# Query and pool-mix products of a decoder trunk as quads of seven block products, interleaved one quad at a time with the attention's units

## The chip, the cores and the metric

The kernel runs on one core of a Trainium2 chip. The metric is the device time of one execution in microseconds (us), the median of several runs. TensorE (PE) multiplies, VectorE (DVE), ScalarE (ACT) and GpSimd (POOL) do elementwise work, SyncE (SP) issues most of the transfers, and 16 DMA engines carry them.

## The reference

One layer with `x` of 2048 tokens by 1024 channels, all in fp32. `c` gives shift, scale and gate through `w_ada`. Then

```
u = x * (1 + scale) + shift
[q | k | v | attn_gate | pool_in | pool_gate | merge_a | merge_p] = u @ W_in
A = SlidingWindowGQA_with_sinks(q, k, v; T5 relative bias) * SiLU(attn_gate)   -> @ W_attn_proj
P = (GroupLinear(MultiScaleCausalPool(pool_in)) * pool_scale) * SiLU(pool_gate) -> @ W_pool_proj
y = (sigmoid(merge_a) * A + sigmoid(merge_p) * P) @ W_out * (1 + gate)
x = LayerNorm(alpha * x + y)
```

The attention has 16 query heads of 64 channels and 2 key heads, with a window of 128 keys that is computed in blocks of 128. The pool averages over the last 2, 4, 8 or 16 tokens, a window for each quarter of the channels.

## The kernel before, in words

**Products.** Every fp32 operand is split into a high part (a copy to fp32r) and a low part (what is left), and a block product is three matmuls for each of four k-tiles: high by high, high by low, low by high (`mm3`, `product`). One block product is thus 12 matmuls of 128x512. A `Quad` is a pair of weight tiles against 1024 tokens. Done plainly it is eight block products; with sums and differences of the blocks (seven products named B11, T1, T2, B21, T3, B22, T4) it is seven. The token side of these seven lies in SBUF as seven sets (`sets`, 2 MB each, high and low). The weight side is a tile `W` of four blocks and a tile `A22`, 1 MB together, which GpSimd turns into sums in place (`sum1` L294, `mid` L298 and L299, `late` L303). ACT and DVE then split them into `w_set` (`pair_split` L325, `half_split` L332, `low` L132), which has four buffers.

**Stages.** The tokens are worked in two halves of 1024, s = 0 and 1. For each half there is a ring (`first_phase` or `second_phase`, run by `ring`) and then an `attention` stage. The ring makes 17 quads two at a time: sixteen gate quads (attn_gate, pool_gate, merge_a, merge_p) and the quad of keys and values. It ends with `first_q`, the plain product of the first query tile. The ring's clock is the tick, one for each block product; `hooks` hang side work on ticks, and a gate's store is put off by two ticks (`defer(2, ...)` in `gate_quad`). At last comes the stage `mix`: attention projection and pool projection of both halves, and the output product with the LayerNorm.

**Attention.** `attention` runs 64 units (head pair by block of 128 queries): scores on PE, bias and maximum on DVE, exponent on ACT, transposes and values on PE. In units 0 to 59 PE also makes half of a plain projection of one 128-channel tile against 512 tokens (`projection`, `parts`): the queries of the next head pair and the pool-mix product. These are plain products, with eight k-tiles and the token sets B11, B21, B22 and, in the set named T2, the raw block B12. The weights of the mix product (`pool_in` folded with the pool's group matrix by `fold_parts`) are kept in DRAM already split (`wmix_d`). Units 60 to 66 open the two quads that the next stage goes on with (`fill_one`). The sums of the pool (`pool_sums`) and the seven block sums of the attention's and the pool's result (`finish`) are made on GpSimd in this stage.

**Side work.** `sums_to` makes the seven sets of the next operand: it loads four blocks into two `spare` rooms, makes four differences on GpSimd, and for each set splits a 128x512 block on ACT (`k_hi`) and DVE (`k_lo`) and stores both (`kept_parts`). `k_hi`, `k_lo`, the gates' `sig` and some others share the five buffers of the tag `c`. In the first ring it does so for the second token half (`u1_d`), in the second ring for `w_out` (`wo_d`), and there `resplit` splits the attention's result of the first half (`ain0_d`). `fill_set` (1 MB a transfer) and `planned` bring sets back. Engines written as `act`, `dve`, `pool`, `sp`, `pe` keep their program order among themselves; `nc.*` calls may be moved by the scheduler.

## Time and profile before

| | us |
|---|---|
| median of 3 runs | 1756.62 (1755.88 to 1757.32) |
| span of the profiled execution, first to last instruction | 1751.3 |
| PE busy | 1697.7 (97%) |
| DVE, ACT, POOL busy | 1205.2, 934.0, 798.3 |
| data moved | 381.31 MB, mean 218 GB/s |

The profiled execution has no other time than its span. The page gives busy time by engine; a view of windows gives the same for a stretch of the span, with the granted clock of TensorE (PEclk, 1.00 is full) and the mean busy share of the 16 DMA engines. Columns of a line that groups instructions: line of the kernel, engine, operation, written and read tiles, shapes, count, busy time, mean of one in ns, and the idle time in front of them with what ended it. Line L56 is that of a helper that keeps the order, so tiles tell the operations apart.

### The profile page before, as it was taken

Reading aid. Unit: us, or ns where it says so; the run is one execution under the profiler, and the core shown is the slowest. Engines: PE = TensorE matmul, PEld = TensorE weight load, DVE = VectorE, ACT = ScalarE, POOL = GpSimd, SP = SyncE. Lnnn points to the kernel's source line nnn. Section 1 sums busy time; section 2 is a strip of 40 time slices with the busy share of each in tenths; the row PEclk is TensorE's granted clock in tenths of the full one; section 3 lists DMA queues with packets and bytes.
Section 4 is the critical chain, followed back from the end, with each engine's and each line's share of the span. In section 5 each row is a group of like instructions: output and inputs, shape, how many; then the busy total and the mean of one; then the engine's idle time right before and its main releaser. Section 6 shows DMA issues by size and latency. Waiting matters only on the chain.

```text
span 1751.3 us, 24998 instructions
## 1 busy us (share of the span) xinstructions
PE 1697.7 (97%) x8248; PEld 1427.4 (82%) x8248; DVE 1205.2 (69%) x2178; ACT 934.0 (53%) x1973; POOL 798.3 (46%) x618
## 2 busy tenths in 40 slices
PE   6899999999999998999999999999999999999996
PEld 5688888878888887888788888888888878887785
DVE  5977665655777777767645357777768696865777
ACT  4644444545777776545444367777745353423452
POOL 2154444441356567434424124555773572463542
PEclk9999999999999999999999999999999999999999
DMA  9384758743354558687777634544698675699432
GB/s 365 117 283 177 276 204 280 257 155 132 114 169 142 178 187 318 237 284 255 276 265 257 234 111 133 180 140 157 232 351 289 185 265 194 216 341 360 157 139 102
DMA packets 185843, 381.31 MB, mean 218 GB/s; under 512 B 18785, under 2 KB 39281, under 8 KB 185713
## 3 DMA queue, kind: packets, MB, share of 16 engines
q1 hardware_dynamic: 179072, 363.92, 59.7%
q0 software_dynamic: 3552, 11.56, 1.7%
q10 hardware_dynamic: 3088, 4.23, 0.8%
q8 instruction: 65, 1.06, 0.2%
q14 instruction: 66, 0.53, 0.1%
HBM read 244.35 MB, written 138.44 MB: 219 GB/s over the span
## 4 chain that ended last, share of the span: by engine, by line
PE 42%; POOL 3%; DVE 2%; DMA 2%; issue 1%; ACT 1%; POOLq 0%; SPq 0%; DVEq 0%; ACTq 0%
PE mm L56 25%; PE lg L56 14%; PE pv L56 2%; PE pt L56 1%; DMA set_T<-ain_T_split 1%; DVE w_set L132 1%; POOL nxt L56 1%; POOL W L298 0%; DVE wide L56 0%; POOL p L56 0%; POOL wide L601 0%; DMA W<-in_wap_dram 0%; POOL rs L56 0%; ACT L L56 0%; POOL a L56 0%
## 5 line engine op out<-in xcount | busy, mean ns | idle before, releaser
L56 PE MATMUL mm<-set_B,w_set 128*128 128x512 f32 x3240 | 799.0, 395 | 12.6 <-ACT u L376 6.3
L56 PEld LDWEIGHTS mm<-set_B,w_set 128*128 128x128 f32 x3240 | 603.2, 189 | 140.7 <-DVE w_set L132 8.8
L56 PE MATMUL lg<-set_T,w_set 128*128 128x512 f32 x2088 | 504.4, 392 | 11.8 <-DVE w_set L132 5.1
L56 PEld LDWEIGHTS lg<-set_T,w_set 128*128 128x128 f32 x2088 | 391.3, 188 | 99.5 <-DVE w_set L132 8.0
L132 DVE TENSOR_TENSOR w_set<-W,w_set 128x1024 fp32r<-128x1024 f32 x162 | 224.0, 1383 | 182.7 <-ACT w_set L325 172.1
L325 ACT CAST w_set<-W 128x1024 fp32r<-128x1024 f32 x162 | 170.6, 1053 | 291.1 <-PE mm L56 221.6
L56 PE MATMUL mm<-set_T,w_set 128*128 128x512 f32 x1080 | 265.6, 394 | 0.0
L56 PEld LDWEIGHTS mm<-set_T,w_set 128*128 128x128 f32 x1080 | 200.7, 188 | 41.1
L294 POOL TENSOR_TENSOR W<-W,A 128x512 f32<-128x512 f32 x56 | 83.8, 1497 | 218.3 <-DMA W<-in_win_dram 59.4
L303 POOL TENSOR_TENSOR W<-W 128x512 f32<-128x512 f32 x56 | 83.5, 1492 | 165.5 <-DVE w_set L132 150.3
L56 DVE TENSOR_TENSOR o<-pv,o 64x128 f32<-64x128 f32 x256 | 72.4, 283 | 88.6 <-ACT o L56 85.5
L56 ACT ACTIVATE L<-L,nm 128x257 f32<-128x257 f32 (+1 forms) x256 | 127.7, 501 | 9.4 <-DVE nm L56 3.9
L298 POOL TENSOR_TENSOR W<-W 128x512 f32<-128x512 f32 x56 | 90.9, 1624 | 78.6 <-DVE w_set L132 68.9
L56 DVE CUSTOM_DVE_ANT_0 L<-lg,bt,nsink 128x256 f32<-128x256 f32 (+1 forms) x256 | 111.6, 473 | 5.0 <-PE lg L56 0.8
L299 POOL TENSOR_TENSOR W<-W 128x512 f32<-128x512 f32 x56 | 88.6, 1582 | 33.6 <-DMA W<-in_win_dram 26.6
L56 POOL TENSOR_TENSOR w_set<-W,w_set 128x1024 fp32r<-128x1024 f32 x14 | 33.7, 2410 | 139.7 <-ACT w_set L56 97.0
L56 POOL TENSOR_TENSOR p<-nxt,pg 128x512 f32<-128x512 f32 x32 | 41.9, 1311 | 107.0 <-DVE sm L56 104.6
L56 ACT COPY o<-pv 64x256 f32<-64x256 f32 x128 | 47.5, 371 | 76.7 <-PE pv L56 76.0
L56 DVE TENSOR_TENSOR ptl<-pt,pth 128x512 fp32r<-128x512 f32 (+1 forms) x128 | 85.8, 670 | 1.9 <-ACT pth L56 1.7
L56 PE MATMUL lg<-kk,qs 128*128 128x256 f32 (+1 forms) x512 | 80.5, 279 | 0.0
L56 ACT ACTIVATE L<-L,sm 128x256 f32<-128x256 f32 (+1 forms) x128 | 64.5, 504 | 30.0 <-DVE sm L56 30.0
L56 DVE TENSOR_TENSOR k_lo<-spare,k_hi 128x512 fp32r<-128x512 f32 x61 | 60.4, 992 | 28.5 <-ACT k_hi L56 13.4
(216 smaller groups left out, 2308.2 us busy)
## 6 DMA issues: line engine op xcount, KB each, us to landing
W<-in_win_dram SPq DMA_DIRECT2D x48, 512.0 KB, 5.2
w_set<-wmix_d SPq DMA_DIRECT2D x32, 512.0 KB, 5.2
W<-in_win_dram SPq DMA_DIRECT2D x34, 256.0 KB, 3.2
A<-in_win_dram SPq DMA_DIRECT2D x34, 256.0 KB, 5.0
ag_d<-sig SPq DMA_DIRECT2D x32, 256.0 KB, 3.9
pg_d<-sig SPq DMA_DIRECT2D x32, 256.0 KB, 3.8
ma_d<-sig SPq DMA_DIRECT2D x32, 256.0 KB, 3.9
mp_d<-sig SPq DMA_DIRECT2D x32, 256.0 KB, 3.8
```

Of the source, the lines that this page charges most:

```text
L56: return lambda *args, **kw: self.tc.keep_in_program_order(op(*args, **kw))
L132: engine.tensor_tensor(dst, src, as32(hi), ALU.subtract)
L294: e.tensor_tensor(self.w[:, 1, :], self.w[:, 2, :], self.a22, ALU.add)
L298: e.tensor_tensor(x[:, 1, :], x[:, 1, :], x[:, 0, :], ALU.subtract)
L299: e.tensor_tensor(x[:, 2, :], x[:, 0, :], x[:, 2, :], ALU.subtract)
L303: e.tensor_tensor(x[:, 3, :], x[:, 3, :], x[:, 1, :], ALU.subtract)
L325: a.copy(by_two(hi), raw)
```

## The change

The plain projections are gone. The query and mix products become quads of seven block products with the sets that the gates use, so that the set T2 stays what it is and B12 is not kept.

- **Ring.** It now makes 10 quads in five groups: eight of attn_gate and pool_gate, the keys and values, and the first query quad. All side work of the rings is placed on these fewer ticks. In the second ring the side work is that of `w_out` as before, the split sums of the attention result of half 0 (`ain0_d`) and the unsplit sums of the pool result (`pin_d[0]`), twelve runs of `sums_to` in all, with eight rooms and starts from tick 3 to 62.
- **Attention.** 13 quads (`fills`: four mix, three query, four merge_a, two merge_p) and the first two products of two more quads are made between the units, in quarters of a block product: 93 products over 67 units, 5 or 6 quarters a unit. The split of each weight block is one 128x512 copy on ACT and one difference on GpSimd, issued three products ahead. Merge gates are stored raw, and their sigmoid is taken when they are read in the last stage. The results of attention and pool are stored raw; their block sums are made later by `sums_to`.
- **After the attention.** The last two merge_p quads (`post`) open a ring of their own, in which the next sets come in (`planned`). T3 and T4 stay in place through the attention.
- **Keys and values.** Only one key head is held at a time; the other lies in DRAM (`k_d`, `v_d`) and is fetched at units 28 to 33.
- **Last stage.** It begins with the two `post` quads of half 1, and eight runs of unsplit `sums_to` for half 1 are spread over its first ticks.
- **Mix weights** are stored unsplit (4 MB in place of 8 MB) by SP in place of GpSimd.

The core of the diff:

```diff
-    def sums_to(ph, store, i, load, work, b12):
-
-        b = []
+    def sums_to(ph, store, i, load, work=None):
+
+        b, split_too = [], store["B11"].shape[0] == 4
...
+        raw = () if not split_too else ((4, "B11", (0, 0)), (5.4, "B21", (1, 0)), (6.1, "B22", (1, 1)))
         for at, name, z in (
-            (4, "B11", (0, 0)), (4.7, "B12", (0, 1)), (5.4, "B21", (1, 0)), (6.1, "B22", (1, 1)),
-            (8.5, "T1", (0, 1)), (10, "T2", (1, 1)), (11.5, "T4", (1, 0)), (13, "T3", (0, 0)),
+            *raw, (8.5, "T1", (0, 1)), (10, "T2", (1, 1)), (11.5, "T4", (1, 0)), (13, "T3", (0, 0)),
         ):
-            if b12 or name != "B12":
+            if split_too:
                 split, keep = kept_parts(ph, store[name][i], lambda z=z: x(*z))
                 todo += [(at, split), (at + 1, keep)]
+            else:
+                todo.append((at + 0.6, lambda name=name, z=z: put(sp, store, name, i, x(*z))))
         return sorted(todo, key=lambda t: t[0])
...
+    def load_raw(store, i):
+
+        def load(x, r):
+            for c in range(2):
+                sp.dma_start(cols(x, c), store[(("B11", "B12"), ("B21", "B22"))[r][c]][i // 2, :, i % 2, :])
+
+        return load
...
+        def block(self, name):
+
+            if name == "T4":
+                return self.a22
+            return self.w[:, {"B11": 0, "T1": 1, "T2": 1, "B21": 3, "T3": 2, "B22": 3}[name], :]
...
-        quads = [kv] if s else []
-        for name, base, kind in (("ag", TAG, "silu"), ("pg", TPG, "scaled"), ("ma", TMA, ""), ("mp", TMP, "")):
+        g = {}
+        for name, base, kind in (("ag", TAG, "silu"), ("pg", TPG, "scaled"), ("ma", TMA, "raw"), ("mp", TMP, "raw")):
             for m in range(0, KT, 2):
-                quads.append(gate_quad(s, name, base, m, kind))
-        last = quads[15:] if s else [kv, quads[15]]
-        return [quads[i : i + 2] for i in range(0, 14, 2)] + [quads[14:15], last], turn
+                g[name, m] = gate_quad(s, name, base, m, "" if (name, m) in (("mp", 4), ("mp", 6)) else kind)
+        def row(name, *ms):
+            return [g[name, m] for m in ms]
+
+        ring_groups = [row("ag", 0, 2), row("ag", 4, 6), row("pg", 0, 2), [kv, q_quad(0)], row("pg", 4, 6)]
+        x = {n: [mk(m) for m in range(0, KT, 2)] for n, mk in (("mix", mix_quad), ("q", q_quad))}
+        ma, mp = row("ma", 0, 2, 4, 6), row("mp", 0, 2)
+        fills = [
+            ("mix", 0, x["mix"][0]), ("ma", 0, ma[0]), ("q", 2, x["q"][1]), ("mix", 2, x["mix"][1]),
+            ("ma", 2, ma[1]), ("q", 4, x["q"][2]), ("mix", 4, x["mix"][2]), ("ma", 4, ma[2]), ("mp", 0, mp[0]),
+            ("q", 6, x["q"][3]), ("mix", 6, x["mix"][3]), ("ma", 6, ma[3]), ("mp", 2, mp[1]),
+        ]
+        return ring_groups, fills, row("mp", 4, 6), turn
...
+        def take_p(m, t, acc):
+            n = pool_free[0] = max(now_n[0], pool_free[0] + 1)
+            x = []
+
+            def first():
+                x.append(ld("pg", gates_d["pg"][s, m, t], 2))
+                x.append(pool_sums(m, t, acc))
+
+            def second():
+                pg, p = x
+                dve.scalar_tensor_tensor(p, p, 1.0 / POOL_W[m // 2], acc, ALU.mult, ALU.subtract)
+                pool.tensor_tensor(p, p, pg, ALU.mult)
+                later(n + 2, lambda: keep_raw(pin_d[s], m, t, p))
+
+            later(n + 1, second)
+            if (m % 2, t) == (0, 1):
+                free_b[0] = n + 1
+            if n == now_n[0]:
+                first()
+            else:
+                later(n, first)
...
+        seq = []
+        for x in range(K):
+            seq += [(x, "T2"), (x, "B21"), (x, "T3"), (x, "B22"), (x + 1, "B11"), (x, "T4"), (x + 1, "T1")]
+        seq += [(K + 1, "B11"), (K + 1, "T1")]
+        splits = {}
+        for i in range(len(seq)):
+            lead = 2 if seq[i] == (K + 1, "B11") else 3
+            splits.setdefault(i - lead, []).append(i)
...
+        def split(i):
+            x, name = seq[i]
+            q = quads[x]
+            if name == "B11" and x > 1:
+                q.sum1(pool)
+            w = ph.split()
+            hi, lo = made[i] = w[:, 0:CH], w[:, CH:]
+            act.copy(hi, q.block(name))
+            low(pool, lo, q.block(name), hi)
+            if name == "T1":
+                q.mid(pool)
+            elif name == "B21":
+                q.late(pool)
+
+        def begun(i):
+            x, name = seq[i]
+            if name == "T1":
+                st[x][1] = bank()
+                if x < K:
+                    later(free_b[0], lambda: seed(x))
+                    if free_b[0] < now_n[0]:
+                        run_coming()
+            if name == "B11":
+                st[x] = [bank(), None, None, None]
+                if x < K:
+                    quads[x + 1].load(ph, False, sp, None)
+            if (x, name) == (K - 1, "B22"):
+                quads[K + 1].load(ph, False, sp, None)
+            for j in splits.get(i, ()):
+                split(j)
+
+        def seed(x):
+            st[x][2] = bank()
+            act.copy(st[x][2], st[x][0])
+
...
+        def filling():
+            for i, (x, name) in enumerate(seq):
+                begun(i)
+                w = made.pop(i)
+                acc = st[x][{"B11": 0, "B21": 0, "T1": 1, "B22": 1}.get(name, 2)]
+                for k in range(4):
+                    product(acc, w, name, name in ("B11", "T1"), k, k + 1)
+                    yield
+                ended(i)
...
-            i = n // 2
-            if i < len(slots):
-                kind, m, st = slots[i]
-                if n % 2 == 0:
-                    accs[kind, m, st], parts[i] = projection(us[st])
-                parts[i](tiles[i // 2][1:], 4 * (n % 2), 4 * (n % 2) + 4)
-            elif n >= 60:
-                fill_one(n)
+            while done < -(-total * (n + 1) // (N + 3)):
+                next(fill)
+                done += 1
...
-        halves_of = [(name, half) for name in set_names[:-1] for half in range(2)]
+        side = []
         for i in range(4):
             ks = (i, 4 + i)
-            todo = sums_to(
+            side.append(sums_to(
                 ph,
                 wo_d,
                 i,
                 lambda x, r, ks=ks: load_wo(x, ks[r]),
                 lambda x, r: dve.tensor_tensor(x, x, cb, ALU.mult),
-                False,
-            )
-            steps(hooks, groups, 5 + 26.5 * i, todo)
-            for n in range(4):
-                if halves_of:
-                    steps(hooks, groups, 19 + 26.5 * i + 2.6 * n, resplit(ph, *halves_of.pop(0)))
-        for half in range(2):
-            hooks.setdefault((-1, 3 + half), []).append(lambda half=half: fill_set("T2", half, u1_d["B12"]))
-        return ring(ph, groups, opened, hooks, [], lambda tick: first_q(ph), True)
+            ))
+        for raw, split in ((ain_d[0], ain0_d), (pin_d[0], pin_d[0])):
+            for i in range(4):
+                side.append(sums_to(ph, split, i, load_raw(raw, i)))
+        ahead, hooks = hooks, {}
+        for start, todo in zip((3, 8, 12, 16, 20, 24, 28, 32, 36, 40, 57, 62), side):
+            for offset, f in todo:
+                at = int(start + offset) - 14
+                if at < 0:
+                    ahead.setdefault((0, at + 14), []).append(f)
+                else:
+                    hooks.setdefault((at // 14, at % 14), []).append(f)
+        later_hooks, hooks = hooks, ahead
+        hooks.setdefault((0, 2), []).append(gate_rows)
+        planned(hooks, ph, u1_d, True)
+        opened = ring(ph, [post], opened, hooks, groups[0], lambda tick: [front(ph, q, tick) for q in groups[0]])
+        hooks = later_hooks
+        planned(hooks, ph, None, False)
+        hooks.setdefault((3, 0), []).append(lambda: ph.turns.clear())
+        turned(hooks, lambda i: turn(ph, i), 4)
+        opened_by = [q for _, _, q in fills[:2]]
+        return ring(ph, groups, opened, hooks, opened_by, lambda tick: [front(ph, opened_by[0], tick)])
...
+        every = [(i, gi) for i, (groups, _) in enumerate(phases) for gi in range(len(groups))]
+        sides = [{} for _ in phases]
+        for n, (raw, i) in enumerate((raw, i) for raw in (ain_d[1], pin_d[1]) for i in range(4)):
+            for offset, f in sums_to(ph, raw, i, load_raw(raw, i)):
+                at = int(2 + 7.5 * n + offset)
+                i, gi = every[at // 14]
+                sides[i].setdefault((gi, at % 14), []).append(f)
...
+    with Pools("g1", spare=4, p=2, c=5) as ph:
+        kq, k, v = rooms_of("second")
+        ph.turns["spare"] = cycle([None, None, *kq, cols2(k, 0), cols2(k, 1)])
+        opened = second_phase(ph, opened, plans[0][2], plans[1])
```

More of the change, by code (lines that the diff above doesn't have):

```diff
@@ L784, in bias_tile, with attention, ld @@
+    def attention(ph, s, fills, post, opened):
+        tp = ph.t
+        run_due(True)
+        quads = [q for _, _, q in fills] + post
+        K = len(fills)
+        def ld(name, src, bufs):
+            x = tp.tile([P, CH], F32, tag=name, bufs=bufs, name=name)
+            sp.dma_start(x, src)
+            return x
         def bias_tile(j):
@@ L922, in attention @@
-        for n in range(N + 5):
+        seed(0)
+        p5 = st[0][3] = tp.tile([P, CH], F32, tag="p5", bufs=2, name="p5")
+        act.copy(p5, st[0][1])
+        for i in range(-3, 0):
+            for j in splits.get(i, ()):
+                split(j)
+        fill = filling()
+        lgs, exps, Ls, pvs, outs, ags = {}, {}, {}, {}, {}, {}
+        total, done = 4 * len(seq), 0
+        for n in range(N + 3):
+            now_n[0] = n
             j, t, b = n // U, n // NB % 2, n % NB
```

517 lines of the change are left out of this document (220 added, 297 removed).

## The prediction

> **What bounds the kernel now.** I read the page first (busy time, costliest groups), then a view of windows by stage, then the chain that ended last, then the transfers.
>
> ```profile
> span 1751.3 us, 24998 instructions
> L56 PE MATMUL mm<-set_B,w_set 128*128 128x512 f32 x3240 | 799.0, 395 | 12.6 <-ACT u L376 6.3
> L56 PE MATMUL lg<-set_T,w_set 128*128 128x512 f32 x2088 | 504.4, 392 | 11.8 <-DVE w_set L132 5.1
> L56 PE MATMUL mm<-set_T,w_set 128*128 128x512 f32 x1080 | 265.6, 394 | 0.0
> ```
>
> The span is 1751.3 us, 5.3 us below the median of the runs (1756.62). I take these 5.3 us as lying around the span and unchanged. The three groups hold 3240 + 2088 + 1080 = 6408 matmuls, 534 block products. Now by stage (columns: length, busy time of PE, PEld, DVE, ACT, POOL, clock, share of the DMA engines, GB/s):
>
> ```profile
> 100.00:413.00 313.00, 310.09 (x1447) 256.99 (x1446) 190.06 (x202) 138.28 (x209) 131.44 (x99) 1.00 0.65 227
> 686.00:700.00 14.00, 7.70 (x29) 6.01 (x28) 6.92 (x11) 5.42 (x9) 10.05 (x10) 0.76 1.00 379
> 700.00:1006.00 306.00, 304.53 (x1346) 251.56 (x1345) 183.39 (x200) 145.52 (x223) 113.68 (x76) 1.00 0.73 258
> 1006.00:1275.00 269.00, 269.00 (x1533) 235.41 (x1532) 193.74 (x605) 199.34 (x587) 137.51 (x107) 1.00 0.50 162
> 1275.00:1325.00 50.00, 49.76 (x233) 41.07 (x232) 30.52 (x47) 21.45 (x38) 29.64 (x25) 1.00 0.91 339
> 1550.00:1600.00 50.00, 50.00 (x222) 41.40 (x221) 26.19 (x25) 12.04 (x15) 23.62 (x18) 1.00 1.04 395
> ```
>
> PE is busy throughout: 310 of 313 us in the first ring, 304.5 of 306 in the second, all of 269 in the second attention. So a block product that goes away is worth its PE time, as long as the others keep up. What matters for them is the last two columns: the second ring already moves 258 GB/s, and the most that 50 us show is 395 GB/s, with the DMA engines busy throughout.
>
> ```profile
> 893.52 2.72 PE lg L56 x12
> 1069.07 2.75 PE mm L56 x12
> 1073.22 2.77 PE mm L56 x12
> ```
>
> From the chain: a block product takes 2.72 us in a ring, 2.75 beside the attention, and a unit of the attention 4.15 us (1073.22 - 1069.07), so 1.40 us of it are the unit's own matmuls.
>
> **What goes: 16 products.** For each token half the queries and mix tiles were 64 plain products (60 in the units, 4 in `first_q`). As eight quads they are 56. Twice 8 products by 2.72 us is **-43.5 us** (518 products, 6216 matmuls). The units' own work stays, and so does the folding.
>
> **The handover after the first attention.**
>
> ```profile
> 686.40 2.91 PE L56 MATMUL lg<-set_T,w_set 128*128 128x512 f32 x12
> 695.61 5.73 PE L56 MATMUL mm<-set_B,w_set 128*128 128x512 f32 x17 [6.30 <-ACT u L376]
> ```
>
> PE idles 6.3 us there, and the next 17 matmuls take 5.73 us instead of 17 x 2.72/12 = 3.85, in the window whose clock is 0.76: 8.2 us in all. T3 and T4 now stay in place, so this wait goes. Late next is the split of the post quads' second pair. Between nothing and all 8.2 us I take **-4 us**.
>
> **The second ring: the same transfers in less time.** The ring had 17 quads as cover for its side work and has 12 now (two of them half done), 82 products or 223 us instead of 306.
>
> ```profile
> set_T<-u_B_split SPq DMA_DIRECT2D x2, 1024.0 KB, 6.7
> W<-in_win_dram SPq DMA_DIRECT2D x17, 512.0 KB, 5.7
> ag_d<-sig SPq DMA_DIRECT2D x16, 256.0 KB, 5.2
> wo_T_split<-k_hi SPq DMA_DIRECT2D x16, 256.0 KB, 2.5
> wo_T_split<-k_lo SPq DMA_DIRECT2D x16, 256.0 KB, 2.4
> spare<-in_wout_dram SPq DMA_DIRECT2D x16, 256.0 KB, 4.4
> ```
>
> These sizes give a tally up to tick 45, where the last split run of `sums_to` ends (starts 3 to 32, each 13 ticks): 14 set fills of 1 MB (`planned`; they came in during the attention before, save T3 and T4), weights of 6 quads, 25 gate stores, loads of ten runs at 1 MB, and 56 splits stored as two pieces of 256 KB (28 from `w_out`, 28 from the attention result). That is 14.7 + 6.3 + 6.6 + 10.5 + 29.4, with the gate rows and the first pool store 68 MB (1024 KB = 1.05 MB). PE needs 47 ticks x 2.72 = 128 us for that stretch, so it asks for **530 GB/s**. At 395 GB/s the bytes take 172 us: 44 us too many. After tick 45 there are 18 MB for 95 us.
>
> A second count points the same way. Every split and every gate needs buffers of the five of tag `c`.
>
> ```profile
> 702.37 0.60 ACT L572 ACTIVATE sig<-mm 128x512 f32<-128x512 f32 x1
> 708.22 0.68 SPq L56 DMA_DIRECT2D ag_d<-sig  x1
> L56 ACT CAST k_hi<-spare x56: 604/622/634, 716.9 to 973.7; 128x512 fp32r<-128x512 f32 x56
>   DMA ma_d<-sig: 6.9, 3
> ```
>
> A gate's buffer lives from 702.37 to 708.22 + 5.2 (landing), 11 us; a split's some 4 us (0.62 copy, 0.7 to 1.0 for the other part, 2.5 landing). Even before, ACT waited for such buffers (6.9 us in three waits for `ma_d<-sig` alone). From tick 7 to 45, 106 us, 112 x 4 + 23 x 11 = 701 us of buffer life fall on five buffers: 140 us, 34 too many.
>
> Can the side work simply run late? The gate stores stand in SP's order behind the stores of the splits of the two ticks after them, so a gate's buffer is not free until the side work has come that far. Five buffers let the ring lead by about two ticks, not by the 16 that 44 us are. So PE's queue stands behind `sig` and `w_set` on ACT. Bounds: nothing (all 86 MB of the ring fit into 223 us at 386 GB/s if everything could be moved) and 68 MB at the second ring's own rate, 258/0.73 x 1.04 = 367 GB/s, 185 us, 57 too many. I take **+40 us**, between the two counts, nearer the bytes.
>
> The Trainium skill ("DMA: Bandwidth & Descriptors", section "Where 436 GB/s comes from") says that transfers between HBM and SBUF are bound by the memory side at some 358 GB/s. The trace disagrees with 395 over 50 us; by the page this term would be 190 - 128 = 62 us and the sum 22 us more.
>
> **The first ring.** Up to tick 44 it carries three runs of `sums_to`, the folding, the gate columns and six quads, 42 MB in (44 - 4) x 2.72 + 25 us of folding = 134 us, 313 GB/s. That is under 395, and PE lost 2.9 us there before (313 - 310.09). **+3 us**, bounds 0 and 10.
>
> **The attention.** 93 products over 67 units make a unit 1.388 x 2.72 + 1.40 = 5.18 us, 347 us a half. The split's low part and the block sums are now GpSimd's:
>
> ```profile
> L56 POOL TENSOR_TENSOR w_set<-W,w_set 128x1024 fp32r<-128x1024 f32 x7 | 16.9, 2409 | 70.7 <-ACT w_set L56 70.7
> L56 POOL TENSOR_TENSOR p<-nxt,pg 128x512 f32<-128x512 f32 x15 | 19.3, 1289 | 52.8 <-DVE sm L56 52.8
> L56 POOL TENSOR_TENSOR nxt<-nxt 128x512 f32<-128x512 f32 x12 | 13.5, 1129 | 0.9
> L299 POOL TENSOR_TENSOR W<-W 128x512 f32<-128x512 f32 x2 | 2.6, 1302 | 0.0
> ```
>
> Lows 93 x 1.20, block sums 56 x 1.30, pool adds 40 x 1.13, products with gates 32 x 1.29: 112 + 73 + 45 + 41 = 271 of 347 us, 78%. It isn't even: the quad of mix tiles 6 and 7 (16 tokens) lasts 26 us and puts 15 + 4 x (4 x 1.13 + 1.29) = 38 us on GpSimd. 12 us queue up in front of a split that is issued three products, 11.2 us, ahead; tiles 4 and 5 queue 8. So PE waits a little, and DVE too, whose `scalar_tensor_tensor` of the pool comes only one unit after the sums: **+6 us** for both halves, between 0 (PE waited for nothing before) and 2 x (12 + 8) = 40. ACT gains 1.4 copies a unit and loses one; at 199.34/64.8 units = 3.1 us of a unit it has room.
>
> **The last stage.** Its first 14 ticks, 38 us, must bring 10 set fills, the weights, the gates and side loads: 10.5 + 2.1 + 2.1 + 3.9 = 18.6 MB, 47 us at 395 GB/s; before, the same place ran at 0.91 with PE at 49.76 of 50. **+6**, bounds 0 and 13. In the pool projection GpSimd has 8 sums of `W`, 8 of these, and 1.87 runs of four differences:
>
> ```profile
> L601 POOL TENSOR_TENSOR wide<-gp,wide 128x512 f32<-128x512 f32 x16 | 27.6, 1729 | 13.3 <-DVE gp L599 13.3
> L56 POOL TENSOR_TENSOR spare<-spare 128x512 f32<-128x512 f32 x16 | 26.6, 1666 | 5.4 <-DVE k_lo L56 2.7 <-issue 2.5
> ```
>
> At some 1.7 us each these are 24 x 1.7 = 40 us in a group of 38. Two groups: **+3**, bounds 0 and 8.
>
> **The sum.** -43.5 - 4 + 40 + 3 + 6 + 6 + 3 = +10.5: a span of 1762 and, with 5.3 around it, **1767 us**.
>
> **The rivals.**
> - *The side work gives way* (the other side). The scheduler may move unordered ring work ahead of the splits; for it speaks that the whole ring's 86 MB just fit. It decides at a lead of more than some four ticks. Then the second ring loses 8 us in place of 40 and the rest stays: 1735. With every term at its lower bound it is 1756.6 - 43.5 - 8.2 = 1705. Against it: the gate stores' place in SP's order. Chance 0.38 (1705 to 1752).
> - *GpSimd bounds the attention.* If its operations take there what they take in the rings, 1.6 instead of 1.3 (the page's L298: 1624), the 271 us are 334 of 347, and every mix quad overruns its lead: some 25 us more, 1792. It decides at about 85% busy. Against it: DVE's work in the attention mostly reads PSUM. Chance 0.14.
>
> ```profile
> L298 POOL TENSOR_TENSOR W<-W 128x512 f32<-128x512 f32 x56 | 90.9, 1624 | 78.6 <-DVE w_set L132 68.9 <-DVE rs L56 9.7
> ```
>
>   The Trainium skill ("GPSIMD Engine Reference", section "1. Specifications") says that GpSimd shares SBUF interfaces with VectorE and contends with instructions that have two SBUF inputs; the 1302 of the attention against the 1624 here agrees.
> - *The products don't fall to 518*, or fall where PE isn't the bound: 1757. Chance 0.02.
>
> My forecast (second ring loses 30 to 55 us, 1753 to 1782) has 0.46. Some 0.2% (3.5 us) is what a measurement can tell from no change. Faster: 0.38 and 0.02 of mine, **0.40**. Within: **0.07**, the lower end of mine and the top of the first rival. Slower: **0.53**. Signs are mixed, so the range, 1718 to 1793, spans both; the forecast's own is 1753 to 1782.
>
> **What would show it.** 6216 matmuls of these groups. In the second ring PE idle of 30 us or more in its first half, behind ACT's waits for `DMA ..._split<-k_lo` or for set fills, at about 0.95 to 1.05 DMA share; next to none in its second half. In the attention a unit of 5.2 us and GpSimd near 78%. No idle at the first handover. It is wrong if the second ring lasts under 240 us, or if PE idles in the attention by more than 15 us a half.

## The result and the profile after

| | before | after |
|---|---|---|
| median of 4 runs, us | 1756.25 (1754.04 to 1757.32) | 1882.11 (1880.76 to 1886.14) |
| span of the profiled execution, us | 1751.3 | 1884.3 |
| mean granted clock of TensorE over the span | 0.993 | 0.958 |

The ratio is 1.0723, with a 95% interval of 1.0705 to 1.074: 126 us slower, where 10 were forecast. The profiled execution after is the slowest of its four, so the spans differ by 133. The page of the kernel after, its head and the three groups of matmuls:

```profile
span 1884.3 us, 24950 instructions
PE 1713.3 (91%) x8056; PEld 1418.5 (75%) x8056; DVE 1231.1 (65%) x2270; ACT 974.2 (52%) x2044; POOL 1062.8 (56%) x810
...
L56 PE MATMUL mm<-set_B,w_set 128*128 128x512 f32 x2664 | 681.0, 403 | 55.4 <-ACT w_set L325 29.7
...
L56 PE MATMUL mm<-set_T,w_set 128*128 128x512 f32 x1824 | 464.0, 401 | 27.8 <-DVE mm L56 12.5
L56 PE MATMUL lg<-set_T,w_set 128*128 128x512 f32 x1728 | 433.4, 402 | 46.0 <-DMA set_T<-u_T_split 15.7
```

2664 + 1824 + 1728 = 6216: the 16 products are gone, as forecast. Two things stand against them: the idle time in the last column (12.6, 0.0 and 11.8 before in the same order; 55.4, 27.8 and 46.0 now), and the mean of a matmul, 401 to 403 ns in place of 392 to 395.

To see where, I cut both traces at the same events: a stage ends with the last value matmul of an attention, and an attention begins with its first score matmul. The products also moved between the stages, so the third column takes before's stage and adds or takes off 2.72 us for each product that came or went (-51, +26, -34, +26, +17).

| stage, us | before | before with the products moved | after | more than the products say |
|---|---|---|---|---|
| first ring | 417.7 | 279.0 | 277.8 | -1 |
| first attention | 268.9 | 339.6 | 363.5 | +24 |
| second ring | 329.2 | 236.7 | 324.5 | +88 |
| second attention | 272.3 | 343.0 | 363.6 | +21 |
| last stage | 463.3 | 509.5 | 554.9 | +45 |

The sum is -43.5 + 177 = +133, the difference of the spans. The second ring, in windows of the kernel after (columns as before: length, busy time of PE, PEld, DVE, ACT, POOL, clock, DMA share, GB/s), and, in the last two lines, the start of the last stage:

```profile
641.00:700.00 59.00, 54.90 (x240) 44.17 (x238) 30.96 (x32) 24.82 (x35) 22.33 (x16) 1.00 0.97 337
700.00:760.00 60.00, 30.38 (x93) 22.11 (x94) 25.06 (x27) 14.49 (x23) 19.38 (x13) 0.72 0.88 301
760.00:850.00 90.00, 58.28 (x197) 43.83 (x197) 55.68 (x56) 35.32 (x57) 43.21 (x28) 0.80 0.80 275
850.00:966.00 116.00, 113.11 (x484) 91.62 (x483) 68.17 (x78) 52.30 (x82) 56.33 (x39) 0.97 0.61 208
...
1329.00:1400.00 71.00, 69.28 (x306) 56.76 (x305) 23.21 (x29) 24.13 (x34) 28.66 (x20) 1.00 0.98 372
1400.00:1600.00 200.00, 174.71 (x704) 138.23 (x704) 128.59 (x117) 86.50 (x115) 129.83 (x78) 0.92 0.75 257
```

Read the second and third lines: 290 matmuls in 150 us, which at 2.72/12 = 0.227 us each need 66. So 84 of the ring's 88 us are lost between 700 and 850 us. Of these, PE was idle for 150 - 88.7 = 61, and the other 23 are matmuls that were busy too long: 88.7 for 290 is 306 ns each, at a clock of 0.72 and 0.80. The timeline shows that directly (start, duration, what, idle time before and its releaser):

```profile
705.79 2.93 PE L56 MATMUL lg<-set_T,w_set 128*128 128x512 f32 x6 [6.97 <-DMA set_T<-u_T_split]
...
714.00 2.92 PE L56 MATMUL mm<-set_B,w_set 128*128 128x512 f32 x6 [5.29 <-DMA set_B<-u_B_split]
...
720.34 2.93 PE L56 MATMUL mm<-set_B,w_set 128*128 128x512 f32 x6 [3.40 <-DMA set_B<-u_B_split]
```

Six matmuls take 2.93 us after such a wait, 488 ns each, about twice the usual 227. A stall is paid for twice, as idle time and as slow matmuls behind it. The Trainium skill ("TensorE: Matmul & The Clock Gate", section "Part 1: The HAM clock gate (the "warmup" mystery)") says that an idle window of about 3.4 us throttles the array to half rate until it has been busy about as long. These rows agree as to the wait and the half rate. The length varies: behind the last of them the next twelve matmuls took 3.11 us, nearly the usual time, while after a wait of 7.79 us at 758 us all twelve were slow (5.89 us).

Who released PE and SP in the second ring (rows: who, for whom, us in total, times, longest):

```profile
POOL W L288 <- DMA A<-in_win_dram: 50.4, 4, 24.8
...
ACT w_set L325 <- POOL W L288: 24.8, 6, 8.0
PE mm L56 <- ACT w_set L325: 24.3, 5, 8.5
...
PE lg L56 <- DMA set_T<-u_T_split: 15.7, 4, 7.0
...
ACT k_hi L56 <- DMA wo_T_split<-k_hi: 11.5, 3, 6.7
...
PE mm L56 <- DMA set_B<-u_B_split: 10.2, 3, 5.3
```

```profile
SPq L56 <- DVE k_lo L56: 56.3, 36, 6.0
SPq L56 <- ACT k_hi L56: 27.9, 22, 4.8
```

PE waits 15.7 + 10.2 = 26 us straight for set fills. The other rows, followed upwards, read as a circle: PE waits for split weights, ACT for GpSimd's sums, GpSimd for the load of `A`. SP issues that load, and it stands in its order behind stores whose `k_lo` and `k_hi` aren't made, because ACT waits until earlier stores have landed and set the buffers free. This chain is a reading of the rows; no experiment follows it link by link. The transfers are slower too (KB each, median us to landing):

```profile
set_T<-u_T_split SPq DMA_DIRECT2D x8, 1024.0 KB, 8.7
...
wo_T_split<-k_hi SPq DMA_DIRECT2D x16, 256.0 KB, 5.8
wo_T_split<-k_lo SPq DMA_DIRECT2D x16, 256.0 KB, 4.6
```

Before, the two kinds of store took 2.5 and 2.4 us, and the three fills of a `set_T` that this ring had took 6.7 us (two from `u_B_split`) and 7.9 us (one from `u_T_split`). But a row of waits alone shows no cause: the kernel before had these two in its second ring as well, and its PE was busy.

```profile
SPq L56 <- DVE k_lo L56: 57.8, 49, 3.8
SPq L56 <- ACT k_hi L56: 54.5, 32, 4.2
```

### The profile page after: what moved, and what is told of

Same layout as the page of the kernel before. It is cut to its first block, busy times and chain, and to the rows that moved or that the text cites. A ratio compares the mean times of both kernels' runs of the same rounds, so it can differ in the third digit from the quotient of the medians.

```text
span 1884.3 us, 24950 instructions
## 1 busy us (share of the span) xinstructions
PE 1713.3 (91%) x8056; PEld 1418.5 (75%) x8056; DVE 1231.1 (65%) x2270; ACT 974.2 (52%) x2044; POOL 1062.8 (56%) x810
## 3 DMA queue, kind: packets, MB, share of 16 engines
q8 instruction: 64, 1.05, 0.2%
## 4 chain that ended last, share of the span: by engine, by line
PE 32%; POOL 6%; DMA 6%; DVE 5%; issue 3%; ACT 1%; SPq 1%; POOLq 0%; DVEq 0%; ACTq 0%
PE mm L56 20%; PE lg L56 10%; DVE w_set L135 1%; PE pv L56 1%; PE pt L56 1%; POOL w_set L56 1%; POOL nxt L56 1%; POOL fin L56 1%; DMA ain_T<-spare 1%; DMA W<-in_wpp_dram 1%; POOL wide L617 1%; ACT w_set L325 1%; DMA spare<-ain_B 1%; DMA A<-in_wap_dram 0%; DMA W<-in_wap_dram 0%
## 5 line engine op out<-in xcount | busy, mean ns | idle before, releaser
L56 PE MATMUL mm<-set_B,w_set 128*128 128x512 f32 x2664 | 681.0, 403 | 55.4 <-ACT w_set L325 29.7
L56 PEld LDWEIGHTS mm<-set_B,w_set 128*128 128x128 f32 x2664 | 508.2, 194 | 176.1 <-ACT w_set L325 33.4
L56 PE MATMUL mm<-set_T,w_set 128*128 128x512 f32 x1824 | 464.0, 401 | 27.8 <-DVE mm L56 12.5
L56 PE MATMUL lg<-set_T,w_set 128*128 128x512 f32 x1728 | 433.4, 402 | 46.0 <-DMA set_T<-u_T_split 15.7
L56 PEld LDWEIGHTS lg<-set_T,w_set 128*128 128x128 f32 x1728 | 333.2, 194 | 125.6 <-ACT lg L368 16.2
L56 PEld LDWEIGHTS mm<-set_T,w_set 128*128 128x128 f32 x1824 | 341.0, 191 | 103.9 <-DVE mm L56 16.9
L56 POOL TENSOR_TENSOR w_set<-W,w_set 128x512 fp32r<-128x512 f32 x160 | 208.8, 1312 | 158.2 <-ACT w_set L56 152.7
L288 POOL TENSOR_TENSOR W<-W,A 128x512 f32<-128x512 f32 x46 | 68.8, 1495 | 314.2 <-ACT sig L585 64.3
L56 POOL TENSOR_TENSOR spare<-spare 128x512 f32<-128x512 f32 x68 | 117.1, 1724 | 28.1 <-DVE spare L56 13.0
L56 ACT CAST pth<-pt 128x512 fp32r<-128x512 f32 (+1 forms) x128 | 72.9, 569 | 81.5 <-PE pt L56 81.0
L56 ACT CAST w_set<-W 128x512 fp32r<-128x512 f32 (+1 forms) x164 | 100.4, 626 | 23.6 <-POOL W L56 10.0
```

The lines of the kernel that those rows point to most:

```text
L56: return lambda *args, **kw: self.tc.keep_in_program_order(op(*args, **kw))
L288: e.tensor_tensor(self.w[:, 1, :], self.w[:, 2, :], self.a22, ALU.add)
```

## The experiments

Each kernel is the kernel after with the edit shown. Unless a range is given, a kernel was run once, beside one run of the kernel before on the same chip: 1752.53 (`r2_buffers`, `ain_raw`, `att_low_half`, `mix_no_sides`), 1756.86 (`r2_buffers_b`, `r2_fill_half`, `r2_fill_act`, `att_one_add`) or 1755.84 (`no_splits`, `att_mult_dve`, `mix_put_late`, `v1`). These single runs lie within 5 us of one another, so a difference of a few us between two kernels is none. The stages of the traces tell more: in runs whose edit leaves a stage as it is, the second ring took 321.9 to 326.2 us, the first attention 360.4 to 366.0, the second 361.7 to 363.6 and the last stage 554.5 to 556.7. The theories, in short: in the second ring, too many bytes, too few buffers, or SP's order; in the attention, the pool's window sums on GpSimd, or GpSimd's load as a whole; in the last stage, the block sums as side work, or the place of their stores.

Six kernels change what is computed. `r2_buffers` and `r2_buffers_b` store split pieces of the second ring that a later split has overwritten (the same number of operations and bytes). `r2_fill_half` doesn't bring the low parts of half 1's sets. `att_one_add` adds up only 2 tokens in every window. `mix_no_sides` stores raw blocks in the place of half 1's block sums. `all_out` has the last two.

**Second ring: more buffers.** Every other split takes its two pieces from the room of the values, which is free there; `r2_buffers_b` does it with a tile of the type fp32r.

```diff
         ph.turns["spare"] = cycle([None, None, *kq, cols2(k, 0), cols2(k, 1)])
+        ph.turns["parts"] = cycle([[cols(v, n).bitcast(F32R) for n in range(2)], None])
```

> Edit: in the second ring every other split uses a room of its own (the idle room of the values) in place of two buffers of tag c; the bytes are the same. The second ring (end of attention 1 to the first score of attention 2) lasts 325 us in the changed kernel, 88 more than its block products explain. Theory A, the five buffers: 56 of 112 buffer uses go, the count by buffers falls below the time of the products, so the ring loses 40 to 60 us of the 88 and the total is 1822 to 1842. Theory B, the bytes: 68 MB still pass in the same stretch, gain at most 10 us, total 1872 or more.

> Edit: as in the first run with a room of its own for every other split, with the room declared in the type of the parts. The same expected: theory A (buffers) 265 to 285 us for the second ring, theory B (bytes) 315 or more; the first run gave 309.

Measured: 1869.73 and 1872.03. The ring takes 309.0 and 310.3 us, 15 less than the 324.5, between what the two theories gave. So buffers are part of it. What enough of them would give isn't shown: the room holds one pair, half of the splits pass through it one after the other, and SP now waits for that pair (`r2_buffers`):

```profile
SPq L56 <- ACT second_vv L56: 30.7, 11, 7.5
...
SPq L56 <- DVE second_vv L56: 14.7, 14, 3.0
```

**Second ring: fewer bytes.** The fills of half 1's sets in that ring bring only the high parts, half of the bytes, with the same number of transfers.

```diff
-    def fill_set(name, half, src, eng=None):
+    def fill_set(name, half, src, eng=None, hi_only=False):
...
+        if hi_only:
+            nc.sync.dma_start(dst[:, :, 0, :], src[2 * half : 2 * half + 2, :, 0, :].rearrange("i p c -> p i c"))
+            return
...
-            return [(p, lambda n=n, h=h: fill_set(n, h, store[n])) for p, n, h in PLAN]
+            return [(p, lambda n=n, h=h: fill_set(n, h, store[n], hi_only=store is u1_d)) for p, n, h in PLAN]
```

> Edit: the 14 set fills of the second ring bring the high parts alone, 7.3 MB instead of 14.7 (the low parts stay those of the tokens before, so the output is not the reference's); buffers and order stay. Theory B, the bytes: 61 MB instead of 68, 18 us less, and 20 to 30 with the slower clock in the stalls: second ring 295 to 305. Theory A, the buffers: at most 10 us, 315 or more.

Measured: 1873.22, ring 309.9 us: 15 less again, between the two theories again. The room that the missing bytes left wasn't filled by others: the same 150 us moved 264 and 284 GB/s in place of 301 and 275, 41 MB in place of 43.

```profile
700.00:760.00 60.00, 38.23 (x124) 28.59 (x122) 34.60 (x35) 19.14 (x30) 29.31 (x19) 0.77 0.78 264
760.00:850.00 90.00, 62.37 (x223) 48.33 (x224) 55.63 (x58) 36.03 (x57) 42.86 (x27) 0.83 0.83 284
```

**Second ring: the fills out of SP's order.** They are issued by ACT.

```diff
-            return [(p, lambda n=n, h=h: fill_set(n, h, store[n])) for p, n, h in PLAN]
+            eng = nc.scalar if store is u1_d else None
+            return [(p, lambda n=n, h=h: fill_set(n, h, store[n], eng)) for p, n, h in PLAN]
```

> Edit: the same fills, whole, are issued by ACT instead of SP. Theory G, SP's order: in the changed kernel SP stands 84 us on k_lo and k_hi before it can issue what is behind them, the fills among them; past SP they come earlier and the second ring falls by 20 to 40 us (285 to 305). Theory B, the bytes: the same transfers share the same engines, 318 to 330. If ACT stands on the sets instead, the stage grows.

Measured: 1875.89, ring 315.4 us, 9 less, again between the theories (285 to 305 and 318 to 330). PE lost more at the start of the ring (46.04 us busy from 645 to 700 us, against 50 to 53 in the kernels above) and less behind it (46.88 us busy from 700 to 760, against 30.38 in the kernel after).

**The attention's result unsplit.** Block sums of half 0's attention result are stored as they are and split when they are read, as the pool's are.

```diff
-        for raw, split in ((ain_d[0], ain0_d), (pin_d[0], pin_d[0])):
+        for raw, split in ((ain_d[0], ain_d[0]), (pin_d[0], pin_d[0])):
...
-            phases.append((pairs(lambda m, s=s: attn_quad(s, m)), ain_d[s] if s else ain0_d))
+            phases.append((pairs(lambda m, s=s: attn_quad(s, m)), ain_d[s]))
```

> Edit: the attention result of half 0 is kept unsplit, as the pool result is; 28 of 56 splits go, with 11 MB of 68 and 56 buffer uses, and the last stage splits seven sets more on ACT and DVE. Theory A, the buffers: second ring shorter by 45 to 65 us. Theory B, the bytes: 57 MB at 395 GB/s are 144 us against 128, so 16 too many in place of 44, a gain of 28 us in that stage. The last stage loses 0 to 10 us by either. Total 1822 to 1842 by A, 1855 to 1860 by B.

Measured: 1838.94, ring 286.7 us, 38 less; the last stage 542.2, 13 less. In the ring that lies between the theories (28 by the bytes, 45 to 65 by the buffers). In the last stage the sets of the attention's result now come in as half of the bytes and are split there. These two stages gain 51 us, the time as a whole 43.

**No splits at all.** As `ain_raw`, and `w_out` too is stored unsplit.

```diff
-    wo_d = split_store("wo")
+    wo_d = set_store("wo")
...
-        raw = () if not split_too else ((4, "B11", (0, 0)), (5.4, "B21", (1, 0)), (6.1, "B22", (1, 1)))
+        raw = () if not (split_too or work) else ((4, "B11", (0, 0)), (5.4, "B21", (1, 0)), (6.1, "B22", (1, 1)))
```

> Edit: both the attention result of half 0 and w_out are kept unsplit, so the second ring stores no split at all; the last stage splits them when it fetches them. Up to tick 45 50 MB remain of 68 (127 us at 395 GB/s, the products' own time), up to tick 18 still 26 MB against 49 us. Theory B, the bytes, with the front-loaded set fills: second ring 245 to 260 us. Theory A, the buffers of tag c alone: 232 to 240. Theory G, SP's order or GpSimd's differences: 270 or more, since the twelve runs and their differences stay. Total about 1795 by B.

Measured: 1788.78, ring 248.9 us, 76 less, so 12 of the 88 are left; that is within the 245 to 260 that the bytes gave, and outside the other two. The last stage takes 536.0 us, 19 less. PE's windows of the ring now:

```profile
640.00:700.00 60.00, 55.83 (x240) 45.39 (x239) 28.54 (x29) 21.57 (x30) 22.62 (x16) 0.97 0.99 366
700.00:760.00 60.00, 51.27 (x196) 39.63 (x196) 24.79 (x28) 16.04 (x24) 37.54 (x27) 0.89 0.95 334
760.00:888.00 128.00, 128.00 (x570) 105.98 (x569) 70.78 (x78) 55.35 (x83) 77.68 (x53) 1.00 0.61 209
```

The ring moves 68.8 MB in place of 86.7, and it does so at 366 and 334 GB/s where the ring with splits did 337, 301 and 275. 18 MB at 395 GB/s would be 45 us. So the splits cost more than their bytes at that rate. With them go their buffers, their stores in SP's order, and the stalls in which the transfers ran below that rate; this run doesn't tell these apart.

**Attention: half of the low parts on DVE.**

```diff
-            low(pool, lo, q.block(name), hi)
+            low(dve if i % 2 else pool, lo, q.block(name), hi)
```

> Edit: in the attention every second weight block has its low part made on VectorE in place of GpSimd. The two attention stages last 363 us each, 21 and 24 more than their products explain. Theory C, GpSimd's queue in the mix quads: 46 operations of 1.3 us leave GpSimd in each, and the stages fall to 340 to 348 us (total 1850 to 1862). Theory D, the one unit between the pool's sums and VectorE's use of them, or VectorE itself: VectorE gets 32 us more in each stage, and the stages stay at 360 or grow (total 1880 to 1895).

Measured: 1893.15, attentions 364.7 and 367.7 us in place of 363.5 and 363.6. GpSimd lost 51 us of work in the first attention (222.51 busy in place of 274.05), and nothing came of it. DVE has 28 us more to do (274.80 busy in place of 246.63), its wait for the pool's sums (the second row) fell from 28.7 us to 10.2, and it waits for ACT's copies in their place:

```profile
DVE w_set L56 <- ACT w_set L56: 35.2, 29, 3.6
...
DVE fin L56 <- POOL fin L56: 10.2, 4, 4.6
```

**Attention: the products with gates on DVE.**

```diff
-                pool.tensor_tensor(p, p, pg, ALU.mult)
+                dve.tensor_tensor(p, p, pg, ALU.mult)
...
-                pool.tensor_tensor(o, o, ags.pop(x), ALU.mult)
+                dve.tensor_tensor(o, o, ags.pop(x), ALU.mult)
```

> Edit: in the attention the two products with gates (32 operations of 1.3 us a half) go from GpSimd to VectorE. Theory C, GpSimd's queue: the mix quads of 16 tokens put 32 instead of 38 us on GpSimd in 26, each stage falls from 363 to 350 to 356 us. Rival, VectorE's in-order waits for GpSimd's sums: 360 or more. Total 1868 by C.

Measured: 1885.03, attentions 360.3 and 360.7 us, 3 less each, hardly beyond the spread of runs that leave these stages as they are; the total shows none of it. As in `att_low_half` DVE's wait for the sums fell, here to 10.1 us from 280 to 640 us, and its own work rose by 28.

**Attention: one addition for each window sum.** Windows of 4, 8 and 16 tokens are worked as 2, so that of the 40 additions of a half 16 are left.

```diff
-            w = POOL_W[g]
+            w = 2
             vb = tp.tile([P, 16 + CH], F32, tag="vb", bufs=1, name="vb")
```

> Edit: every pool window is made as 2 tokens in the attention, so that 24 of GpSimd's 40 adds a half are left out (the output is not the reference's). Theory C, GpSimd's sums of the long windows fill its queue: the stalls go, and each attention stage falls from 363 to 342 to 350 us, total 1855 to 1862. Theory D, the distance of one unit between sums and use, or the seed of the next quad, whatever the length: 358 to 363 us, total 1875 or more. Halving the low parts on GpSimd had left the stages where they were, but it gave VectorE 32 us, so it did not tell the two apart.

Measured: 1850.68, attentions 343.2 and 345.2 us: 20 and 18 less, which leaves 4 and 2 us over the products. First the kernel after, its first attention; then this one:

```profile
277.80:641.30 363.50, 348.17 (x1839) 297.71 (x1838) 246.63 (x704) 237.74 (x658) 274.05 (x227) 0.98 0.34 110
```

```profile
DVE fin L56 <- POOL fin L56: 28.7, 9, 6.5
...
PE mm L56 <- DVE mm L56: 6.9, 2, 4.8
```

```profile
280.00:623.00 343.00, 340.32 (x1838) 292.33 (x1838) 244.16 (x704) 238.64 (x658) 248.23 (x203) 1.00 0.36 117
```

```profile
DVE fin L56 <- POOL fin L56: 2.3, 3, 0.9
```

DVE waited 28.7 us for the sums, and 2.3 now. GpSimd lost 24 additions and 26 us (274.05 to 248.23), half of what `att_low_half` took off it for nothing. So the chain through the window sums carries nearly all of the loss. That GpSimd's work as a whole doesn't count isn't shown, since the two edits that moved some of it gave it to DVE.

**Last stage: no side sums.** Attention stores each raw block of half 1 a second time where a block sum would be, and the eight runs of `sums_to` go.

```diff
+            if s == 1:
+                put(sp, store, (("T3", "T1"), ("T4", "T2"))[m % 2][t], m // 2, x)
...
-        for n, (raw, i) in enumerate((raw, i) for raw in (ain_d[1], pin_d[1]) for i in range(4)):
+        for n, (raw, i) in ():
```

> Edit: the eight runs of sums for half 1 are left out of the last stage; the attention stores the raw block a second time in the place of each sum, so the output is not the reference's. The last stage lasts 555 us, 45 more than its products explain. Theory E, the side runs (GpSimd's differences and their place in SP's order): the stage falls by 30 to 45 us, total 1837 to 1852. Theory F, the sigmoid that ACT now takes on freshly loaded merge gates: the stage falls by 15 us at most, total 1867 or more.

Measured: 1851.9, last stage 519.5 us, 35 less. Its window against the last line of the kernel after above:

```profile
1400.00:1600.00 200.00, 195.69 (x849) 159.65 (x848) 152.63 (x138) 102.43 (x133) 91.13 (x57) 0.99 0.71 232
```

849 matmuls in place of 704 in the same 200 us: 145 x 0.227 = 33 us, nearly all of the gain, in the stretch where the side sums stood.

**Last stage: the stores of the sums one tick later**, so that SP stands less behind GpSimd.

```diff
-                todo.append((at + 0.6, lambda name=name, z=z: put(sp, store, name, i, x(*z))))
+                todo.append((at + (1.6 if ph.name == "mix" else 0.6), lambda name=name, z=z: put(sp, store, name, i, x(*z))))
```

> Edit: in the last stage each store of a sum is placed one tick later in the program, so that SP stands less on GpSimd's differences. Theory E1, SP's order (stores waiting for the difference hold back weights and gates behind them): last stage 530 to 545 instead of 555. Theory E2, GpSimd's time itself: 552 to 558.

Measured: 1879.59, last stage 551.3 us. That is short of the 530 to 545 of SP's order, and only 3 us under what runs with an untouched last stage took, so little if anything was gained.

**A version put together**: `no_splits`, `att_mult_dve` and `mix_put_late`.

> Edit: the three edits together (no splits in the second ring, gate products on VectorE, stores one tick later in the last stage). If the terms add, 279 + 352 + 250 + 352 + 520 = 1753 us of span, the kernel before (1751) within a few us; if GpSimd alone bounds the last stage, 1770.

Measured: 1781.03, a span of 1779.3: 101 us faster than the kernel after, 25 slower than before, and more than either sum expected (1753 and 1770). Its ring took 249.8 us as expected, its attentions 359.3 and 361.3 in place of 352, its last stage 530.3 in place of 520.

**All three loads out**: `no_splits`, `att_one_add` and `mix_no_sides` together, with the edits shown there.

> Three edits together, each of which has been run alone or nearly so: no splits and set stores of split pieces in the rings' side work, window sums of one addition for every pool quad (so the pool's result is left out for the long windows), and no block sums of half 1's results in the last stage (raw blocks stored in their place). If the three losses are separate and are all that holds the saving back, the stages add up to 277 + 343 + 249 + 345 + 505 (536.0 less the 35.4 that the side sums were worth, to 501 to 506) = 1719 us of span, 1721 us of time, about 36 us under the kernel before, with PE busy 98% or more outside the handovers. If the loss is one shared resource, or each removal only uncovers the next wait, the gains don't add: 1740 or more. If PE's own clock or pace were what is slower in the changed order, 1750 or more.

Measured: a median of 1732.24 us in 4 runs (1727.19 to 1734.85) against 1755.16 in 7 of the kernel before, ratio 0.9875 (0.9858 to 0.9891). The stages are 277.8, 341.7, 242.4, 345.5 and 517.9 us, with PE at work nearly without a break in the attentions:

```profile
280.00:624.00 344.00, 342.17 (x1852) 294.33 (x1853) 246.51 (x704) 238.74 (x658) 249.24 (x204) 1.00 0.36 120
624.00:873.00 249.00, 238.52 (x1033) 194.12 (x1032) 126.62 (x144) 100.10 (x157) 149.54 (x101) 0.98 0.76 274
873.00:1218.00 345.00, 344.10 (x1874) 296.36 (x1872) 251.29 (x699) 238.10 (x641) 239.57 (x190) 1.00 0.44 146
```

Once its price is taken out, 22.9 us of the saving are there. The median is 11 us over the 1721 expected, between the two outcomes that I had set. In the profiled execution, the fastest of the four with a span of 1725.4, four stages come within 7 us of their terms; the last stays at 517.9 in place of 505, hardly less than the 519.5 of `mix_no_sides`, so there the gains of the unsplit reload and of the side sums don't add. This kernel leaves work out, so it isn't one to use, and the kernel before was not run with the same work left out. No version that computes everything beat the kernel before.

## Why the prediction was right in sign and wrong in size

- **The products, -43.5: right.** 6216 matmuls. The first ring, +3 within 0 and 10: it took 1 us less than the products say.
- **The handover, -4:** it is in the ring's figure. The timeline of the kernel after has products back to back across the cut at 641 us, and the first window of the ring is at a clock of 1.00, so the 6.3 us of idle time and the slow matmuls behind them are gone, as the sign said. The gain came nearer to the 8.2 us of the term's bound.
- **The second ring, +40 with bounds 0 and 57: the place right, the term mis-sized.** It came to 88, and to 96 if the handover's gain of 8 is taken off first. PE stalled where the forecast said, up to 850 us (61 us idle from 700 on), behind the waits that it named, and hardly in the rest of the ring (113.11 of 116 us busy). What failed is the step "At 395 GB/s the bytes take 172 us". The bytes were right (86.7 MB in the ring, 86 forecast), the rate was not: the windows up to 850 us carry 63 MB, and the 68th passes near 870, some 228 us from the ring's start, at 300 GB/s. A rate seen when every transfer had been issued in time (the window of 50 us with the DMA engines at 1.04) can't be taken for a stretch in which the issuing queue waits for the engines that wait for the transfers. The share of the DMA engines tells it: 0.88 and 0.80, not the 0.95 to 1.05 that the forecast gave as its sign. By these shares the DMA engines were not the bound by themselves, and bytes and buffers, which the forecast counted one beside the other, look to have worked on each other. The clock is no further term on top of this, but it is part of how the loss shows: 23 of its 84 us are slow matmuls, which the forecast of idle time alone didn't have. No experiment found a single part that carries the loss: 15 us for one more pair of buffers, 15 for half of the fills' bytes, 9 for the order of the fills, but 38 and 76 when half and then all of the splits went with their bytes, buffers and stores. How much of the 76 belongs to each stays open.
- **The attention, +6 with bounds 0 and 40: the right place, the wrong end.** It came to 24 + 21 = 45, and PE idled 15.3 us in the first (363.5 - 348.17), just over the 15 that the forecast had set as a sign of being wrong. The forecast found the quads of long windows with 38 us of GpSimd work in 26 and 12 us too many, and then let the lead of 11.2 us take it up. The failed step is "12 us queue up in front of a split that is issued three products, 11.2 us, ahead": the lead shields the splits, but not DVE, which stands in its program order at the use of the sums while other work queues behind it. In one such stretch of the kernel after, GpSimd has hardly a gap. DVE waits for its sums, and PE then stands still until DVE gets to `mm`, an addition between the products of the quad (first the window, then two rows of DVE and one of PE):

```profile
566.00:592.00 26.00, 21.20 (x110) 18.19 (x110) 12.35 (x34) 13.51 (x41) 25.22 (x23) 0.93 0.32 100
...
582.56 0.69 DVE L56 SCALAR_TENSOR_TENSOR fin<-fin,mm 128x512 f32<-128x512 f32 x1 [4.91 <-POOL fin L56]
...
586.28 0.68 DVE L56 TENSOR_TENSOR mm<-mm,p 128x512 f32<-128x512 f32 x1
...
587.02 1.65 PE L56 MATMUL mm<-set_T,w_set 128*128 128x512 f32 x3 [4.80 <-DVE mm L56]
```

  The three matmuls behind that wait take 550 ns each. The upper bound, 2 x (12 + 8) = 40, came near the 45. GpSimd's work was priced well as a whole: 112 + 73 + 45 + 41 = 271 us against 274, with some 1.3 us for a difference or a product. Not separated is whether the full GpSimd of those 26 us or DVE's order is what one would have to change. `att_low_half` and `att_mult_dve` free about 5 of the 12 us there by the forecast's count, which may be too little, and load DVE with it.
- **The last stage, +9 with bounds 0 and 21: mis-sized.** It came to 45. The forecast priced the side sums in two groups of the pool projection, +3, and the stage's start, +6. The start cost next to nothing: the 306 matmuls from 1329 to 1400 us need 69.4 of its 71 us. The failed step is "Two groups: +3": the side sums cost 35, in 1400 to 1600 us. `ain_raw` gained 13 us, but in its trace the same first 71 us of the stage hold 303 matmuls, so the 13 lie behind the start too; and without the side sums the unsplit reload gains almost nothing more (519.5 and 517.9), so 13 and 35 overlap. Some 10 us of the 45 are left without side sums, and their cause is open. In the waits of the kernel after for 1329 to 1700 us those for weights, for gates and for the sums stand beside each other:

```profile
POOL W L288 <- DMA A<-in_wap_dram: 41.1, 4, 18.5
...
ACT gp L614 <- DMA gp<-mp_d: 30.8, 8, 7.7
```

```profile
SPq L56 <- POOL spare L56: 51.2, 12, 9.0
```

  SP waits for the sums before it stores them, and the weights and gates behind those stores come late. That reading is argued from the rows. `mix_put_late` tried to ease it and gained little if anything, so which part of the side sums costs the 35 (SP's order, their loads, or GpSimd's time beside DVE) stays open.
- **The rivals.** That the side work gives way (0.38) fell: PE stalled, as the gates' place in SP's order spoke for. That GpSimd bounds the attention (0.14) was nearer in place than the forecast, but its mechanism, operations of 1.6 us, didn't come (1.30).
- **The sum.** The terms other than the products were put at 54 us and came to 177: 52 more in the ring with its handover, 39 more in the attentions, 36 more in the last stage, 4 less in the first ring. Three terms lay above their upper bounds, so the range was too narrow for more than one reason; in the ring, both bounds were worked out with transfer rates that the trace of before had only shown without a stall. The sign was right, but at a chance of 0.53 and with a sum of 10 between terms of 40, that is a small success. Two slips of the forecast bear on nothing above: a ring that loses 30 us gives 1757 and not 1753, and only 64 of the 67 units have the 1.40 us of matmuls of their own, so an attention is 343 us by its count and not 347.

## What to carry to other kernels

Where work is packed into fewer steps, count the transfers, the buffer lives and the orders of the queues for the stretch, and then don't take the best rate ever seen: here a ring of engines, queue and buffers that waited for each other ran its transfers at 300 GB/s where 395 had been seen, and the 61 us of stalls brought another 23 of slow matmuls. Where an engine is over its time for a short stretch, ask not only whether its own consumer has a lead but which in-order engine stands waiting for it, and what else that engine serves. A saving on a busy engine is worth its full price only if the work that used to lie in its shadow still has a shadow to lie in.

## What the runs showed of the hardware

- Behind waits of PE of 3.40, 5.29 and 6.97 us the next six matmuls took 2.93 us, 488 ns each in place of 227; over the 150 us of the stall, with the clock at 0.72 and 0.80, that was 23 us.
- A 256 KB store of `k_hi` landed 5.8 us after its issue in the second ring of the kernel after, and 2.5 before, though the two rings move nearly the same on average (267 and 258 GB/s by the view of the transfers).
- GpSimd's differences of two 128x512 blocks in `spare`, in the last stage, took 1.82 us, against 1.30 for those in `W` in the first attention:

```profile
L56 POOL TENSOR_TENSOR spare<-spare 128x512 f32<-128x512 f32 x32 | 58.1, 1817 | 0.5
```

```profile
L56 POOL TENSOR_TENSOR W<-W 128x512 f32<-128x512 f32 x40 | 51.3, 1297 | 2.0
```
